# A hybrid decoder layer on one core: moving token sums, output rows, banks, norm weights and the closing order

## The chip, the core and the metric

The kernel runs on one core of one Trainium2 chip. A core has a tensor engine for matrix products (PE, with its weight loads shown apart as PEld), a vector engine (DVE), a scalar engine (ACT), a general engine (POOL) and a synchronisation engine (SP) that here only issues transfers. Each engine works through its own list of instructions in order; an instruction starts when the semaphores that it waits for are there. Transfers between main memory and the chip's memory are issued from the lists of SP, ACT and POOL. Products go into accumulation banks: eight of them, each 128 partitions by 512 float32 numbers.

The metric is the device time of one execution in microseconds (us), as the median of several runs. The times of the kernel before were 1899.18 (median of three), 1897.68 (lowest) and 1900.45 (highest).

## The reference

The reference is one layer: a token mixer with two kinds of heads, then a gated feed-forward network (FFN) with a short convolution over time, each behind a norm and added to the stream. All is float32. There are 1024 tokens of width 1024, with 16 learned tokens (`meta`) ahead that are dropped at the end. Cut to what matters:

```python
def rms_norm(x, g):
    return x * lax.rsqrt(jnp.mean(x * x, axis=-1, keepdims=True) + EPS) * g

def mixer_block(h, ...):                       # h: 1040 x 1024, normed with norm_mix
    proj = h @ w_in + b_in
    (g_q, g_k, g_v, g_r, g_lr, m_q, m_k, m_v, m_o, m_i, m_f, gate_a, gate_b) = jnp.split(proj, ...)
    log_a = jax.nn.log_sigmoid(g_lr @ gla_w_gate + gla_b_gate) / 16      # decay, per key column
    o_gla = head_rms(gla_chunked(g_q, g_k, g_v, log_a), gla_norm) * jax.nn.silu(g_r)   # 4 heads
    mq, mk = jnp.split(jax.nn.silu(causal_dwconv(concat(m_q, m_k), ml_conv_w, ml_conv_b)), 2)
    o_ml = head_rms(mlstm_chunked(mq, mk, m_v, m_i, log_sigmoid(m_f)), ml_norm) * jax.nn.sigmoid(m_o)
    y = jax.nn.sigmoid(gate_a) * (o_gla @ w_branch_gla) + jax.nn.sigmoid(gate_b) * (o_ml @ w_branch_ml)
    return y @ w_out

def conv_ffn(h, ...):                          # 2816 columns of gate and of up
    gate, up = jnp.split(causal_dwconv(h @ w_up, conv_w, conv_b), 2)
    return (jax.nn.silu(gate) * up) @ w_down

h = concat(meta, x)
h = h + mixer_block(rms_norm(h, norm_mix), ...)
h = h + conv_ffn(rms_norm(h, norm_ffn), ...)
return rms_norm(h, norm_final)[16:]
```

The two scans run over chunks of tokens; the first kind of head (GLA) decays its state per key column, the second (mLSTM) by scalar gates.

## The kernel before

**Numbers.** A float32 number is split into a rounded high part and the difference, a low part (names ending in H and L). A product of two numbers is three products: high by high, high by low, low by high. So each weight unit is loaded (`wr_`, or `raw`), rounded on ACT into `wH` and subtracted on DVE into `wL`. For the mixer this is `prep` (L104). It has two places for raw weights and three for each half. `U.get` fetches units in their order of use. `hold(ins)` makes the ACT rounding of the next units stand behind the instruction `ins` in ACT's list.

**Order.** The program is written in one stream, and a planner puts each instruction into its engine's list, by default in program order. `hp(n)` moves instructions ahead by up to n places. `tc.issue_after(ins)` puts what follows behind `ins` if it is on the same engine; that is an order, not a wait between engines. A tile with a tag shares its place with the other tiles of that tag, and a new one waits until an old one has been read.

**Start (L292 to L376).** `idle_products(8, "a")` (L338) gives PE eight products of `ident` by itself (two matrix instructions each). SP's list loads the meta rows and the first tile of x (`load_x(0, 1)`), then `norm_mix` spread over 128 partitions by the transfer itself (`gmix`, 512 KB), then the second tile of x. `norm_x(i)` (L305) norms tile i: squares with a sum on ACT, mean and root on DVE and POOL (`xr`, the root L316), one scaling by root and `gmix` on DVE (L317), eight transposes on PE (L322) in two banks, then for each bank a rounding on ACT and a subtraction on DVE into `xH` and `xL`. The squares go into a scratch tile with tag "of". After the last tile, POOL builds the masks of the scan (L379 to L407), behind the last root.

**Heads (s = 0 to 7, GLA first).** `key_query_proj` (L423) projects keys (`pk`) and queries (`pq`). For s = 0 it yields six pieces of the keys of heads 0 and 1 and the queries, then the small projection `lr` (decay and gate rows, into `raw_s`), then a piece, then `decay(0)` (L623: products, then ACT and DVE on `la` and a scan into `bc`, L637 and after), then the rest, and then puts head 0's scan `gla(0)` into the side stream, with its copies of the keys on POOL (`pk`, L712 and after). `small_rows` (L525) makes the mLSTM gate rows around head 3, with operations on few partitions by 1040 columns. `post(s)` (L585) scales a head's output and transposes it out.

**Work put beside the heads.** `token_sums(k)` (L472), k = 0 to 3, forms sums and differences of token halves for two blocks of columns: eight POOL operations of 128 by 514 in two tiles of tag "of", then eight stores of 132 KB on POOL's own queue. The gate stage (L1150 and after) reads them. It runs at the start of `post(s)` for s = 3 to 6, behind the last root on POOL. `half_load` (L501) and `half_sums` (L511) take one half of a block of `w_down`, form four differences on POOL and store them for the last stage. One half runs in each `post(s)` for s = 3 to 5, with the load behind the stores of the token sums; others in the gate stage and the merge:

```python
            for _ in range((2, 2, 1, 1, 0)[q - NK]):     # L1191, gate stage
                half_sums(*half_load(gs, "o0"))
```

**Gates, merge, output.** The merge (L1262 to L1307) multiplies the heads' outputs by the branch weights, `prod3`, in two tiles of three banks each (`big`), which DVE reads (`sb`, L1297). Then come the output products (`po`, L1520): for token tiles of 128 rows and four column blocks n of 256, `y @ w_out`. Tile 0 stands for the two rows of meta tokens that the convolution needs. `yH` and `yL` are the split rows of y, in eight blocks of 128 columns, the last of which is ready last:

```python
    for i, tiles in enumerate(([1, 5, 2, 6, 0], [3, 7, 4, 8])):
        for n in range(4):
            for u in uo[i][n]:
                U.get(u)
```

So the weights of the output (eight units of 512 KB each time) are loaded and split twice, once for each list of tiles. The first three tiles of n = 0 run together in banks X1, V0 and X0: first all but the last block of y, then the last block. `out_sum` (L1525) adds each result to the stream on DVE and squares it on ACT. At n = 3 `norm2a` norms a finished tile, and `second_norm` (L1502), which runs one or two tiles later, scales, transposes and splits it; tiles 3 and 7 and then 4 and 8 make the second piece of the FFN's tokens (`second_piece`, `combos`), whose sums and differences (L1354 to L1396) must be there before the second products of the FFN. The last `second_norm` calls stand inside the first piece of the FFN.

**FFN and end.** The up projection multiplies in seven products instead of eight, over pieces U, V, X, Y and Z (L1001). The down projection runs in rounds r and column blocks j (L1669, banks `banks[r, j, x]`). After the last of a block, `finish(r, j)` (L1745) adds the banks to the stream (`accs`), squares, roots and scales by `norm_final` (`gfin`). `whole(i)` (L1761) takes root and scaling of half a block and its store. For the end block (1, 1), the second half goes through `fo` in two column halves, the first scaled on ACT, the second on DVE, and the first half last:

```python
        nc.vector.tensor_scalar(fo[:, hi], fo[:, hi], rs, None, OP.mult)
        nc.sync.dma_start(out[P * t:P * (t + 1), hi], fo[:, hi])
        whole(0)
```

## Time and profile before

| | |
|---|---|
| median of the runs | 1899.18 us (1897.68 to 1900.45) |
| the profiled execution | 1897.74 us |
| its span in the trace | 1895.8 us |
| mean granted clock of PE | 0.996 of full speed |
| instructions | 32688 |
| read from and written to main memory | 198.33 and 69.57 MB, 141 GB/s over the span |

The profile is of one execution, with times in microseconds. A line that groups instructions names the line of the kernel, the engine, the operation, and out<-in by the program's names, then partitions x elements and types. In a list in order of time the first number is the start, the second the duration (of all x instructions that stand together), and in square brackets stand the engine's idle time just before and what ended it. A line of waits says who waited, in which group, for which engine and group, and then the total, the number and the longest. In a table of windows, the stretch is followed by its length, by the busy time of PE, PEld, DVE, ACT and POOL with the number of instructions, by the granted clock, the share of the transfer engines, and GB/s. A line for a group with three times behind it gives the shortest, the mean and the longest of one in ns, and then from when to when they ran. A busy engine is only busy; whether the time counts is told by the waits of the engine that sets the end.

### The profile page before, as it was taken

To read this page: it belongs to the slowest core of one execution; us is meant where nothing else is said; L and a number is where in the kernel's file an instruction comes from. 1 tells how busy PE (TensorE), PEld (TensorE's weight loads), DVE (VectorE), ACT (ScalarE), POOL (GpSimd) and SP (SyncE) were. 2 spreads that over 40 slices of the span, in tenths; PEclk is the share of its full clock that TensorE was granted. 3 is DMA by queue.
4 is the path that set the end of the run, shared out by engine and by line. 5 is a ranking of instruction groups with operands and counts; after the bars stand their busy time and mean duration, and the time that the engine had idled before them with its cause. 6 is when DMAs were issued, how large, how long until landed. Compare 5 with 4: busy or idle time off the path is not lost. (4 is left out here: it accounts for less than half of the span.)

```text
span 1895.8 us, 32688 instructions
## 1 busy us (share of the span) xinstructions
PE 1859.8 (98%) x13377; PEld 1779.6 (94%) x13377; DVE 1214.4 (64%) x1781; ACT 854.0 (45%) x1369; POOL 424.5 (22%) x471
## 2 busy tenths in 40 slices
PE   8999999989999999999999999999999999999998
PEld 8999999989999999999999999999999999987876
DVE  6745646455653376665442556688788788796876
ACT  5454555635543443332332325544343443465664
POOL 3201101244332001124462610012222222200000
PEclk8999999999999999999999999999999999999999
DMA  5111021062243757665883653323433334288794
GB/s 169 34 37 59 16 66 48 23 160 70 79 122 86 202 118 162 159 171 175 302 269 119 215 174 112 129 85 107 132 113 101 106 112 128 84 307 331 276 369 170
DMA packets 221824, 270.02 MB, mean 142 GB/s; under 512 B 13742, under 2 KB 177088, under 8 KB 221675
## 3 DMA queue, kind: packets, MB, share of 16 engines
q1 hardware_dynamic: 200603, 199.93, 34.8%
q0 software_dynamic: 16928, 57.76, 9.6%
q10 hardware_dynamic: 4144, 10.26, 1.5%
q8 instruction: 105, 1.72, 0.4%
q14 instruction: 44, 0.36, 0.1%
HBM read 198.33 MB, written 69.57 MB: 141 GB/s over the span
## 5 line engine op out<-in xcount | busy, mean ns | idle before, releaser
L512 POOL TENSOR_TENSOR ts<-ts 128x256 f32<-128x256 f32 x88 | 80.4, 921 | 55.8 <-DMA ts<-in_ffn_w_down_dram 53.9
L1433 POOL TENSOR_TENSOR SB<-SA,rg 128x512 f32<-128x512 f32 x20 | 32.1, 1605 | 233.8 <-issue 114.1
L206 PE MATMUL pv<-wH_mv,xH 128*128 128x256 f32 x256 | 74.9, 293 | 1.9 <-DVE v L210 1.8
L1520 PE MATMUL po<-wH_wo,yH 128*128 128x256 f32 x256 | 72.8, 285 | 2.5 <-DVE yM L1301 2.4
L206 PE MATMUL pv<-wH_gv,xH 128*128 128x256 f32 x256 | 74.7, 292 | 0.0
L206 PE MATMUL pv<-wL_gv,xH 128*128 128x256 f32 x256 | 72.0, 281 | 0.0
L206 PE MATMUL pv<-wH_gv,xL 128*128 128x256 f32 x256 | 72.0, 281 | 0.0
L1520 PE MATMUL po<-wL_wo,yH 128*128 128x256 f32 x256 | 71.7, 281 | 0.3 <-DVE wL_wo L112 0.3
L1520 PE MATMUL po<-wH_wo,yL 128*128 128x256 f32 x256 | 72.0, 282 | 0.0
L206 PE MATMUL pv<-wL_mv,xH 128*128 128x256 f32 x256 | 72.0, 281 | 0.0
L206 PE MATMUL pv<-wH_mv,xL 128*128 128x256 f32 x256 | 71.9, 281 | 0.0
L721 POOL TENSOR_TENSOR pk<-pk,kT 128x256 f32<-128x256 f32 (+1 forms) x24 | 32.8, 1368 | 147.9 <-ACT pk L719 140.3
L1468 DVE SCALAR_TENSOR_TENSOR cv<-u,fc,cv 128x1024 f32<-128x1024 f32 x44 | 65.3, 1484 | 0.4
L1415 POOL TENSOR_TENSOR A<-u2raw,A 128x512 fp32r<-128x512 f32 x20 | 43.9, 2193 | 91.8 <-ACT A L1414 91.8
L1233 PE MATMUL bg<-ogL,wH_bg 128*128 128x342 f32 x192 | 61.5, 320 | 0.0
L1233 PE MATMUL bm<-omH,wH_bm 128*128 128x342 f32 x192 | 61.4, 320 | 0.0
L1233 PE MATMUL bg<-ogH,wL_bg 128*128 128x342 f32 x192 | 61.4, 320 | 0.0
L1233 PE MATMUL bg<-ogH,wH_bg 128*128 128x342 f32 x192 | 61.4, 320 | 0.0
L1233 PE MATMUL bm<-omH,wL_bm 128*128 128x342 f32 x192 | 61.3, 319 | 0.0
L1233 PE MATMUL bm<-omL,wH_bm 128*128 128x342 f32 x192 | 61.2, 319 | 0.0
L1758 POOL TENSOR_TENSOR fr<-fv,mhalf 128x1 f32<-128x1 f32 x8 | 5.6, 711 | 226.5 <-DVE fv L1756 226.5
L210 DVE TENSOR_TENSOR v<-pv,bB 128x256 f32<-128x256 f32 x64 | 26.4, 418 | 44.1 <-PE pv L206 44.0
(754 smaller groups left out, 7518.7 us busy)
## 6 DMA issues: line engine op xcount, KB each, us to landing
gw<-in_w_in_dram SPq DMA_DIRECT2D x26, 512.0 KB
ts<-in_ffn_w_down_dram POOLq DMA_DIRECT2D x44, 256.0 KB, 3.8
tdn<-ts POOLq DMA_DIRECT2D x44, 256.0 KB, 3.5
rg<-in_ffn_w_up_dram SPq DMA_DIRECT2D x22, 512.0 KB
ru<-in_ffn_w_up_dram SPq DMA_DIRECT2D x22, 512.0 KB
adr<-s SPq DMA_DIRECT2D x40, 256.0 KB
rd<-in_ffn_w_down_dram SPq DMA_DIRECT2D x20, 512.0 KB
do<-tdn SPq DMA_DIRECT2D x18, 512.0 KB
```

The costliest lines, as they stand in the source:

```text
L206: nc.tensor.matmul(pt[:, :DV], a[:, k, t0:t0 + P], b[:, k % 4, :], start=(i == 0), stop=(i == 3 * NK - 1))
L210: nc.vector.tensor_tensor(vt[:n, c, :DV], pt[:n, :DV], bB[:n, :], OP.add)
L512: nc.gpsimd.tensor_tensor(t[:, o], t[:, a], t[:, b], OP.subtract)
L721: eng.tensor_tensor(e, e, k, OP.mult)
L1233: nc.tensor.matmul(pt[:, i, :n], a[:, k, :], b[k][:, base + t0:base + t0 + n], start=(k == 0 and j == 0), stop=(k == NK - 1 and j == 2))
L1415: eng.tensor_tensor(l, src, h.bitcast(F32), OP.subtract)
L1433: late.tensor_tensor(sb[:, 0:4], sa[:, 0:4], rg[:, 0:4], OP.subtract)
L1468: nc.vector.scalar_tensor_tensor(y, u[:, j:SEQ + j], fc[:, j, jj:jj + 1], y, OP.mult, OP.add)
L1520: nc.tensor.matmul(pt[:, :DV], a, b[:, k % 4, :], start=(k == 0 and i == 0), stop=(k == NK - 1 and i == len(terms) - 1))
L1758: nc.gpsimd.tensor_tensor(rs, v, mhalf, OP.pow)
```

## The change

It has five parts.

**Start.** `gmix` is no longer spread by a transfer. A 4 KB load of `norm_mix` into one partition (`g1`) stands first on ACT's queue, and two products of one row of ones by 512 columns of it, behind the idle products on PE, spread it over 128 partitions; DVE copies them into `gmix`. There are four idle products instead of eight. The mean of tile 2 is ordered behind the copies on DVE, the squares of tiles 3 and 4 behind the second rounding of tile 2 on ACT, and those of each later tile i behind that of tile i - 2. `prep` now puts its DVE subtraction behind the held instructions too, and the first weight unit is held behind tile 2's scaling, the second behind its rounding.

**Token sums.** The first two sets run inside `key_query_proj(0)`, behind the `lr` projection and ahead of `decay(0)` in the program, with their stores on SP's queue; the other two run in `post(4)` and `post(5)` on POOL's queue. The halves of `w_down` in `post` now run for s = 3 to 6, and the gate stage does one less.

**Banks.** Three empty tiles claim the banks V1, Y1 and Z1 ahead of the output products.

**Output rows.** The list [3, 7, 4, 8] becomes [3, 7] and [4, 8], and the units of `w_out` are loaded and split three times.

**Closing.** `whole` is split into root and `scaled`. In the second round the two scalings stand behind the sums of the block. In the end block the first half's root comes early, its sum is multiplied by `gfin` into a tile `f0`, and then scaled in two column halves, one on ACT early and one on DVE at the end, and stored from there.

The diff, cut to its core:

```diff
@@ -73,6 +73,10 @@
+    g1, ones = (hd.tile([P, T + 3], F32, name=n, tag="k", bufs=2) for n in ("g1", "ones"))
+    nc.vector.memset(ones[0:1, :P], 1.0)
+    nc.scalar.dma_start(g1[0:1, :D], bass.AP(tensor=norm_mix.tensor, offset=norm_mix.offset, ap=[[D, 1], [1, D]]))
+
     ident = const.tile([P, P], F32, name="ident")
     make_identity(nc, ident)
@@ -107,9 +111,11 @@
         wH = wp.tile(shape, F32R, name="wH_" + name, tag="wH")
         wL = wp.tile(shape, F32R, name="wL_" + name, tag="wL")
-        with tc.issue_after(held[0]) if held else nullcontext():
+        with ExitStack() as stack:
+            for ins in held:
+                stack.enter_context(tc.issue_after(ins))
             nc.scalar.activation(wH, raw, AF.Copy)
-        nc.vector.tensor_tensor(wL, raw, wH.bitcast(F32), OP.subtract)
+            nc.vector.tensor_tensor(wL, raw, wH.bitcast(F32), OP.subtract)
         return wH, wL
@@ -302,19 +308,26 @@
             xts.append(xt)
...
-    def norm_x(i):
+    def after(*ins):
+        stack = ExitStack()
+        for i in ins:
+            stack.enter_context(tc.issue_after(i.ins))
+        return stack
+
+    def norm_x(i, *order):
         n = NM if i == 0 else P
         c0 = 0 if i == 0 else NM + P * (i - 1)
...
         ss = hd.tile([P, 1], F32, name=f"xss{i}", tag="ss1", bufs=3)
         junk = hd.tile([P, T], F32, name=f"xj{i}", tag="of", bufs=2)
-        nc.scalar.activation(junk[:n, :D], xt[:n, :D], AF.Square, accum_out=ss[:n])
-        with hp(40):
+        with after(*order):
+            nc.scalar.activation(junk[:n, :D], xt[:n, :D], AF.Square, accum_out=ss[:n])
+        with hp(40), after(*order):
             v = hd.tile([P, 1], F32, name=f"xv{i}", tag="xv", bufs=3)
             nc.vector.tensor_scalar(v[:n], ss[:n], 1.0 / D, EPS, OP.mult, OP.add)
             rs = hd.tile([P, 1], F32, name=f"xr{i}", tag="xr", bufs=3)
             last = nc.gpsimd.tensor_tensor(rs[:n], v[:n], mhalf[:n], OP.pow)
-        nc.vector.scalar_tensor_tensor(xt[:n, :D], xt[:n, :D], rs[:n], gmix[:n], OP.mult, OP.mult)
+        scaled = nc.vector.scalar_tensor_tensor(xt[:n, :D], xt[:n, :D], rs[:n], gmix[:n], OP.mult, OP.mult)
         for g in range(2):
             tp = ps.tile([P, 4, P], F32, name=f"xtp{i}_{g}", tag="pj" if i == 1 else "s", bufs=3)
@@ -325,7 +338,7 @@
                 l4 = xL[:, 4 * g:4 * g + 4, c0:c0 + n]
                 nc.vector.tensor_tensor(l4, tp[:, :, :n], h4.bitcast(F32), OP.subtract)
-        return last, rounded
+        return last, rounded, scaled
...
     fc = const.tile([P, 4, 44], F32, name="fc")
@@ -339,18 +352,26 @@
         pt = ps.tile([P, P], F32, name=f"idle{name}", tag="ot", bufs=2)
         for _ in range(n):
-            nc.tensor.matmul(pt, ident, ident, start=True, stop=True)
-
-    idle_products(8, "a")
+            last = nc.tensor.matmul(pt, ident, ident, start=True, stop=True)
+        return last
+
+    idle = idle_products(4, "a")
     for dst, ap in small[:4]:
         nc.scalar.dma_start(dst, ap)
     load_x(0, 1)
-    nc.sync.dma_start(gmix, rowb(norm_mix, 0, D))
     load_x(2)
+    for i in range(2):
+        tp = ps.tile([P, 512], F32, name=f"gm{i}", tag="s", bufs=3)
+        with tc.issue_after(idle.ins):
+            nc.tensor.matmul(tp, ones[0:1, :P], g1[0:1, 512 * i:512 * i + 512], start=True, stop=True)
+        spread = nc.vector.tensor_copy(gmix[:, 512 * i:512 * i + 512], tp)
     norm_x(0)
     norm_x(1)
+    last, rounded, scaled = norm_x(2, spread)
+    made = [rounded]
+    hold(scaled.ins)
     U.get(0, 0)
-    hold(norm_x(2)[1].ins)
+    hold(rounded.ins)
     U.get(1, 0)
     hold()
@@ -359,13 +380,14 @@
     U.get(2, 0)
     columns()
-    norm_x(3)
+    made.append(norm_x(3, rounded)[1])
     load_x(6, 7, 8)
-    norm_x(4)
+    made.append(norm_x(4, rounded)[1])
     for dst, ap in small[9:]:
         nc.sync.dma_start(dst, ap)
     for i in range(5, NC + 1):
-        last, _ = norm_x(i)
+        last, rounded, _ = norm_x(i, made[i - 4])
+        made.append(rounded)
     conv_columns()
     for t, c in ((xH, 0), (xL, 32)):
@@ -433,6 +455,8 @@
                 yield from proj_cm(uk["lr"], TH_ALL, 0, lambda p, t0, n: nc.scalar.activation(
                     raw_s[0:96, t0:t0 + n], p[0:96, :], AF.Identity, bias=bsm[0:96]))
+                for k in range(2):
+                    token_sums(k, nc.sync)
                 pkq = together(pk, pq)
                 yield from islice(pkq, 1)
@@ -469,7 +493,7 @@
     tsc = [dram.tile([4, P, 4, n], F32, name=f"tsc{n}") for n in (258, 256)]
...
-    def token_sums(k):
+    def token_sums(k, queue):
...
         a, b = ([t[:, :514], t[:, 520:1034]] for t in (
@@ -490,7 +514,7 @@
         for i, src in enumerate((b[0], b[1], a[1], a[0])):
             for p in range(2):
-                stored = nc.gpsimd.dma_start(tsc[p][i, :, k], src[:, 258 * p:258 * p + 258 - 2 * p])
+                stored = queue.dma_start(tsc[p][i, :, k], src[:, 258 * p:258 * p + 258 - 2 * p])
         return stored
@@ -586,9 +610,10 @@
         h = s % 4
         g = "g" if s < 4 else "m"
-        if 3 <= s < 7:
-            with tc.issue_after(rooted[0].ins):
-                stored = token_sums(s - 3)
+        after = rooted[0]
+        if s in (4, 5):
+            with tc.issue_after(after.ins):
+                after = token_sums(s - 2, nc.gpsimd)
         for c in range(NC):
             nc.scalar.activation(o(c), o(c), AF.Copy, scale=sc[:, c + 1:c + 2])
@@ -604,9 +629,9 @@
                 if gi == 0:
                     yield
-                    if 3 <= s < 6:
+                    if 3 <= s < 7:
                         if j == 0:
-                            with tc.issue_after(stored.ins):
+                            with tc.issue_after(after.ins):
                                 t = half_load(wp, "gst")
                         else:
@@ -1188,7 +1213,7 @@
             behind_ = g
         if q >= NK:
-            for _ in range((2, 2, 1, 1, 0)[q - NK]):
+            for _ in range((2, 1, 1, 1, 0)[q - NK]):
                 half_sums(*half_load(gs, "o0"))
     next(behind_)
@@ -1220,7 +1245,7 @@
     ubm = [u_cm(w_bm, P * j, f"bm{j}") for j in range(NK)]
     uo = [[[U.add(wsrc(w_o, 4 * g, 4, DV * n, DV), [P, 4, DV], f"wo{i}{n}{g}") for g in range(2)]
-           for n in range(4)] for i in range(2)]
+           for n in range(4)] for i in range(3)]
...
     def prod3(u, X, kouter, name, ahead=2, base=0):
@@ -1535,8 +1560,11 @@
         return psF.tile([P, 512], F32, name=f"po{n}_{t}", tag=tag)
...
-
-    for i, tiles in enumerate(([1, 5, 2, 6, 0], [3, 7, 4, 8])):
+    for tag in ("V1", "Y1", "Z1"):
+        po_bank("x", tag, tag)
+
+
+    for i, tiles in enumerate(([1, 5, 2, 6, 0], [3, 7], [4, 8])):
         for n in range(4):
             for u in uo[i][n]:
@@ -1745,6 +1773,8 @@
         acc = acc_of(r, j)
         end = (r, j) == (1, 1)
+        if end:
+            f0 = rb.tile([P, T], F32, name="f0", tag="T12")[:, :D]
         ss = [const.tile([P, 2], F32, name=f"fss{r}{j}{i}", tag=f"fs{i}", bufs=2) for i in range(2)]
@@ -1758,8 +1788,7 @@
             return rs
...
-        def whole(i):
-            rs = root(i)
+        def scaled(i, rs):
             nc.vector.scalar_tensor_tensor(acc[i], acc[i], rs, gfin, OP.mult, OP.mult)
             t = 4 * i + 2 * r + j
@@ -1773,15 +1802,21 @@
             add(acc[0], hi, banks[r, j, "Y"])
             square(0, 1)
-            if not end and r:
-                whole(0)
+            if end:
+                rs0 = root(0)
+                nc.vector.tensor_tensor(f0, acc[0], gfin, OP.mult)
+                nc.scalar.activation(f0[:, lo], f0[:, lo], AF.Copy, scale=rs0)
+            elif r:
+                rs0 = root(0)
             add(acc[1], lo, banks[r, j, "Z"])
             square(1, 0)
             if not end:
                 if r:
-                    whole(1)
+                    rs1 = root(1)
+                    scaled(0, rs0)
+                    scaled(1, rs1)
                 else:
-                    later.append(whole)
+                    later.append(lambda i: scaled(i, root(i)))
                 return
         rs = root(1)
@@ -1790,7 +1825,9 @@
         nc.vector.tensor_scalar(fo[:, hi], fo[:, hi], rs, None, OP.mult)
         nc.sync.dma_start(out[P * t:P * (t + 1), hi], fo[:, hi])
-        whole(0)
+        t = 2 * r + j
+        nc.vector.tensor_scalar(f0[:, hi], f0[:, hi], rs0, None, OP.mult)
+        nc.sync.dma_start(out[P * t:P * (t + 1), :], f0)
...
     AHEAD, PRI_F = 4, 100
```

## The prediction

> **What bounds the kernel now.** I read the busy times first, then TensorE's waits, then windows and the time-ordered lists of the stages in which those waits lie.
>
> ```profile
> span 1895.8 us, 32688 instructions
> PE 1859.8 (98%) x13377; PEld 1779.6 (94%) x13377; DVE 1214.4 (64%) x1781; ACT 854.0 (45%) x1369; POOL 424.5 (22%) x471
> ```
> TensorE (PE) is busy for all but 36 us. A change that leaves its products alone can win only from those 36 us, or add to them. The waits of PE, longest first (total, times, longest):
>
> ```profile
> PE xtp L322 <- DVE xt L317: 4.2, 4, 2.7
> PE pj L163 <- DVE v L210: 2.6, 2, 1.5
> PE po L1520 <- DVE yM L1301: 2.4, 1, 2.4
> PE pv L206 <- DVE v L210: 1.8, 2, 1.0
> PE rtp L578 <- ACT of L604: 1.7, 1, 1.7
> PE sc L672 <- DVE pk L722: 1.6, 1, 1.6
> PE Vu L1001 <- DVE BL1r L1396: 1.1, 1, 1.1
> PE Xu L1001 <- ACT u2raw L1030: 0.7, 1, 0.7
> PE htp L1375 <- DVE hs L1354: 0.5, 1, 0.5
> PE Zu L1001 <- ACT BH1t L1395: 0.2, 1, 0.2
> ```
> The first row is the start, the third the first output tiles, the last four the passage to the FFN; rows two, four and five lie beside the small rows of the heads (part 2). Each part of the change aims at one of these or at the tail after the last product.
>
> The sum is made against the profiled execution: 1897.74 us, of which 1895.8 is the span. That is 1.44 us under the median 1899.18, so I add 1.44 at the end.
>
> **Part 1: norm weights by products, fewer warming products, rows in order.**
>
> ```profile
> 1.83 3.78 PE L342 MATMUL idlea<-ident 128*128 128x128 f32 x16 [1.83 <-POOL ident masks.py:199]
> 6.96 2.47 DVE L317 SCALAR_TENSOR_TENSOR xt<-xt,xr,gmix 16x1024 f32<-16x1024 f32 x2 [0.32 <-DMA gmix<-in_norm_mix_dram]
> 10.51 1.28 DVE L317 SCALAR_TENSOR_TENSOR xt<-xt,xr,gmix 128x1024 f32<-128x1024 f32 x1 [0.53 <-POOL xr L316]
> ```
> Four warming products end at 1.83 + 1.89 = 3.7 us. One of 128 columns takes 2 x 0.236 us (3.78 / 16), so a spread product of 512 columns takes about 1.9 and two 3.8: PE is through at 7.5. A copy of 512 columns on DVE is about half of a 1024-wide operation, 0.7 us: the weights stand at 8.2, 1.2 us later than now (6.96). Three scalings at some 1.2 us then end at 11.8, which is when the third ends now (10.51 + 1.28). Today the third comes 1 us after the second, for its rows land late; those come earlier when the 512 KB of spread weights no longer go ahead of them on SP's queue. What follows on DVE is the same work. The rounding of the third tile no longer stands behind the fourth tile's squares on ACT: I give that 0.2 us. The 4 KB load goes first on ACT's queue, where the first squares wait for rows anyway. The later tiles' squares now stand behind a rounding of two tiles earlier, up to 3 us later by my estimate; PE has the earlier tiles' columns to work on, so I cost it at nothing, and that cover is part of the upper bound. **-0.2**, bounds -1.5 (of the four xt waits all but the longest go, 4.2 - 2.7) and +1.5 (the 1.2 us are not caught up).
>
> **Part 2: token sums 0 and 1 move.** Now, beside the small rows:
>
> ```profile
> 372.00:390.00 18.00, 14.20 (x106) 13.27 (x104) 17.78 (x12) 7.12 (x12) 17.89 (x12) 1.00 0.03 10
> 377.19 2.23 DVE L851 SCALAR_TENSOR_TENSOR kc<-kT,col,kc 128x1040 f32<-128x1040 f32 x1
> 381.58 2.33 DVE L547 TENSOR_TENSOR sr<-sr,sr 4x1040 f32<-4x1040 f32 x1
> 390.85 1.30 DVE L851 SCALAR_TENSOR_TENSOR kc<-kT,col,kc 128x1040 f32<-128x1040 f32 x1
> 401.31 1.06 ACT L111 ACTIVATE wH_mv<-wr_mv 128x1024 fp32r<-128x1024 f32 x1 [2.06 <-DMA wr_mv<-in_w_in_dram]
> L478 POOL TENSOR_TENSOR xa<-xH,xL x12: 1282/1296/2329, 372.8 to 572.5; 128x514 f32<-128x514 f32 x12
> ```
> POOL and DVE (the columns are PE, PEld, DVE, ACT, POOL) are both full; the same DVE operation takes 2.23 us beside the sums and 1.30 after them, and a 1040-wide one 2.33 where L637 below takes 1.24. Six operations like these lose about 1 us each, 5.6 us over some 16 us of sums, and PE's waits on v (2.6 + 1.8) come behind them. The 1.7 at L578 stands behind ACT, which waits for a weight load (last but one row) that is under way together with the sums' 1 MB of stores. These 6.1 us should nearly go. What is late next: the half load now starts at once, and its four subtractions on POOL fall beside the same rows; I leave 1.3 us. **-4.8**, bounds -6.1 and -2 (the half sums and the scans of the rows keep two thirds). The sixteen stores of the two sets leave POOL's queue for SP's. In the later heads one set of sums less runs, in places where the list has no wait of PE: 0. The seventh head's added half takes POOL time that the fourth set gives up there: 0. One half less in the gate stage, where PE never waits for POOL: 0.
>
> At the first keys:
>
> ```profile
> 38.30 1.29 POOL L398 TENSOR_SCALAR_AFFINE_SELECT mfs<-mfs 128x64 f32<-128x64 f32 x2
> 61.86 1.24 DVE L637 TENSOR_TENSOR la<-bc,la 128x1040 f32<-128x1040 f32 x1 [3.06 <-ACT la L636]
> 67.09 2.08 POOL L712 COPY pk<-kT 128x256 f32<-128x256 f32 x2 [27.49 <-ACT kT L420]
> 68.36 0.38 SPq L107 DMA_DIRECT2D wr_gq<-in_w_in_dram  x1
> 73.79 1.13 PE L672 MATMUL sc<-pk 128*128 128x128 f32 x8 [1.65 <-DVE pk L722]
> 77.14 1.05 ACT L111 ACTIVATE wH_gq<-wr_gq 128x1024 fp32r<-128x1024 f32 x1
> ```
> POOL is free for 27.5 us. Two sets of eight operations at 1.29 us are 20.6 us. The masks are held behind the last tile's root, which comes about 4 us later (part 1), so they end nearer 44 than 39.6, and the second set ends at 64 to 65, beside DVE's decay chain that begins at 61.86 and for which PE already waits 1.65 us. About 4 us of sums beside it, at the loss seen above (5.6 in 16), cost **+1.5**; bounds 0 (done by 61.8) and +5 (the second set waits until the first one's stores have left its rows, runs to 70 and holds up the copies of 67.09 as well). The 16 stores go on SP. Behind them stands the weight load of 68.36, which may slip by some microseconds: it is split at 77.14, so 0.
>
> **Part 3: banks.**
>
> ```profile
> 1102.78 1.23 DVE L1297 TENSOR_TENSOR sb<-bm,sb 128x1026 f32<-128x1026 f32 x1 [2.88 <-PE bm L1233]
> 1115.81 0.51 DVE L1297 TENSOR_TENSOR sb<-bm,sb 128x342 f32<-128x342 f32 x1
> 1116.46 0.36 PE L1520 MATMUL po<-wH_wo,yH 128*128 128x256 f32 x1 [2.39 <-DVE yM L1301]
> 1118.65 1.29 DVE L1305 TENSOR_TENSOR yL<-sb,yH 128x512 fp32r<-128x512 f32 x2 [0.70 <-ACT yH L1304]
> ```
> PE starts right after DVE's third read of the last merge product (1115.81 + 0.51), out of the three banks that the first tiles take. With V1, Y1 and Z1 claimed ahead, these tiles get the next three, which DVE has read by 1104. Their first 63 products use no last row of yH and take 63 x 0.118 = 7.4 us (price in part 4); the last row is split by 1120, so nothing is late next. **-2.35**, bounds -2.4 and 0 (the banks stay).
>
> **Part 4: output rows two by two.** Eight more weight units: each a 512 KB load, one ACT and one DVE operation.
>
> ```profile
> L111 ACT ACTIVATE wH_wo<-wr_wo x16: 1042/1046/1065, 1091.7 to 1208.3; 128x1024 fp32r<-128x1024 f32 x16
> L112 DVE TENSOR_TENSOR wL_wo<-wr_wo,wH_wo x16: 1203/1214/1225, 1093.8 to 1209.4; 128x1024 fp32r<-128x1024 f32 x16
> 1175.00:1223.00 48.00, 47.18 (x400) 46.70 (x399) 33.56 (x54) 23.88 (x51) 2.52 (x4) 1.00 0.44 138
> PE po L1520 <- DVE wL_wo L112: 0.3, 1, 0.3
> ```
> A product costs PE 47.18/400 = 0.118 us, a tile of 24 products 2.83, a pair 5.7. With three places for each weight half, a pair's second unit can be split only when the unit three before it is free, 1.4 us ahead of the handoff, and it is wanted 1.4 us behind it: 2.8 us for 1.05 on ACT, 1.21 on DVE and the signals. So a handoff has about 0.3 us to spare. The ones of before cost 0.3 us all together. But DVE goes from 33.6 to 33.6 + 8 x 1.21 = 43.3 of 48 us, so that an operation of 0.7 to 1.3 us is often ahead. I take 0.4 us for each of the seven closer handoffs, less the 0.3: **+2.5**; bounds 0 and +10.5 (1.5 each, a whole operation ahead on DVE and part of one on ACT). In return tiles 3 and 7 are normed while 4 and 8 are multiplied. That takes those tiles' scalings, halvings of differences and subtractions, by the durations above about 8 us, from DVE in the passage, whose waits of PE are 1.1 + 0.7 + 0.5 + 0.2 = 2.5. They should go but for 0.5, since the first FFN weights are split later than before: **-2.0**, bounds -2.5 and 0.
>
> **Part 5: closing.**
>
> ```profile
> 1884.12 2.25 PE L1669 MATMUL pdZ<-do,dy 128*128 128x512 f32 x9
> 1890.01 0.49 DVE L1791 TENSOR_SCALAR fo<-fo,fr 128x512 f32<-128x512 f32 x1 [0.66 <-POOL fr L1758]
> 1890.57 1.28 DVE L1763 SCALAR_TENSOR_TENSOR accs<-accs,fr,gfin 128x1024 f32<-128x1024 f32 x1
> ```
> PE ends at 1886.37; behind it stand a sum, squares, a root and two scalings, then a store. The last scaling shrinks from 1.28 to 0.49 (-0.8), but a multiplication of 1.2 us enters DVE's queue earlier, and one half of it a scaling on ACT, where the last squares must not stand behind it. The two scalings of the block before move behind its sums. **-0.3**, bounds -0.9 and +1.2 (the multiplication stands ahead of the last sum).
>
> **Sum:** -0.2 - 4.8 + 1.5 - 2.35 + 2.5 - 2.0 - 0.3 = -5.65: 1892.1 for the profiled execution, **1893.5** as a median.
>
> **Rivals.**
> *The keys take it back.* DVE's decay chain pays the full +5 instead of +1.5: -2.15, 1897.0. For it: PE waits there already. Against: 27 us of idle POOL. The Trainium skill, "SBUF — State Buffer", section "SBUF: two separate sides", says that DVE operations with two SBUF inputs and GpSimd lock each other out for a whole instruction; the 2.23 against 1.30 us agrees.
>
> *The weights bind (slower).* At the pair handoffs of part 4 the stall is 1.5 us each: 7 x 1.5 - 2.5 = +8, and the passage gains nothing, +2: 1893.5 + 10 = 1903.5. It decides from 1.43 us a handoff. For it: DVE would be at 90% in this stage. Against: the handoffs of before cost 0.3 in all.
>
> *The banks do not move.* Claiming empty tiles shifts nothing: 1893.5 + 2.35 = 1895.9.
>
> *The clock stays up.*
>
> ```profile
> 8.00:10.00 2.00, 1.18 (x11) 1.09 (x12) 1.72 (x4) 1.15 (x2) 0.08 (x1) 0.78 1.19 313
> 18.00:20.00 2.00, 2.00 (x13) 2.00 (x13) 1.27 (x3) 0.00 (x0) 0.55 (x1) 0.66 1.03 418
> ```
> With a clock of 1 or 0.5, the means 0.78 and 0.66 (the last column but two) put the fall at 9.1 and the return at 19.4. The dense products, from about 15.7 on, run at half rate for 3.7 us; spread products that bridge the idle time before 8 us could save that half, 1.8: 1891.7. The Trainium skill, "TensorE: Matmul & The Clock Gate", Part 1, has PE's activity judged in free-running windows of about 3.4 us; 19.4 - 9.1 is three of them. By that rule fewer warming products could as well leave it cold longer.
>
> **How the numbers follow.** Runs of this kernel tell about 0.2%, 3.8 us, from no change: faster is under 1895.4, slower over 1903.0. Forecast 0.46 and clock 0.08 make faster 0.54. Keys 0.15, banks 0.07 and smaller misses at the start, the close and the handoffs 0.05 make 0.27 within. Weights 0.19 are slower. All bounds at once would reach from 1885.8 to 1915.4; I take 1888 to 1904, which leaves out the upper half of the weights case, 0.1, and 0.05 below. The forecast's own range is 1889.5 to 1895.4.
>
> **What would show it.** Part 1: the first dense key product starts within 0.5 us of where it does now. Part 2: PE's waits on v (L210) fall under 1.5 us in all, DVE is back at 1.3 us beside the small rows, and the sc wait near 72 us is about 3 us. Part 3: the 2.4 us wait at the first output tile is gone. Part 4: PE's waits on wL_wo total 2 to 3 us, those on the second token piece (L1395, L1396) under 0.6. Part 5: 9.2 us instead of 9.4 from the last product to the end of the span. I am wrong if the wL_wo waits pass 6 us, the sc wait passes 5, or the first output tile still waits for the merge.

## The result, and the profile after

The changed kernel takes 1903.96 us (median of ten runs, 1902.51 to 1909.33), the kernel before 1899.39 (1897.68 to 1901.88): a ratio of 1.0027, 95% interval 1.0017 to 1.0036. It is slower by 0.27%, where 1893.5 was forecast; the time lies just inside the stated range (1888 to 1904) and far above the forecast's own (1889.5 to 1895.4). The profiled execution of the changed kernel took 1904.08 us, with a span of 1902.4; that is 6.6 us more span than before.

The page's first lines:

```profile
span 1902.4 us, 32743 instructions
PE 1863.4 (98%) x13373; PEld 1781.3 (94%) x13373; DVE 1212.3 (64%) x1793; ACT 862.0 (45%) x1378; POOL 409.4 (22%) x455
```

PE's longest waits, with total, number and longest:

```profile
PE ftp L348 <- DVE fc L349: 6.4, 1, 6.4
PE xtp L335 <- DVE xt L330: 4.2, 4, 2.2
PE htp L1400 <- DVE hn L1385: 2.8, 2, 2.0
PE idlea L355 <- POOL ident masks.py:199: 1.8, 1, 1.8
PE Vu L1026 <- ACT BH1r L1420: 1.7, 1, 1.7
PE sc L697 <- DVE pk L747: 1.7, 1, 1.7
PE ot L627 <- ACT of L629: 1.6, 1, 1.6
PE po L1545 <- DVE wL_wo L118: 1.5, 3, 0.8
```

Three things are gone as forecast: the waits on v (2.6 + 1.8), the one at the small rows (1.7) and the one at the first output tile (2.4). The list has a new head: 6.4 us for a copy into `fc`, a small table of the FFN's convolution weights that nobody would look for on the path. And `htp` now waits 2.8 us for `hn`, where the passage to the FFN had waited 2.5 in all.

Waits do not add up to 6.6 us, so I compared when PE starts the same product in both traces. How much later the changed kernel is:

```
product                                     before     after    later by
first key product                            13.88     14.56      0.68
106th key or query product                   36.71     38.39      1.68
121st                                        38.49     48.93     10.44
first product of the scan (sc)               73.79     85.35     11.56
head 3, just before the small rows          319.05    330.64     11.59
first product of the mLSTM scan (msc)       426.15    430.38      4.23
first gate product (Vg)                     658.73    662.80      4.07
first product of the last b gates (pe)      921.04    926.23      5.19
first output product (po)                  1116.46   1119.10      2.64
553rd output product                       1187.28   1189.81      2.53
FFN, 89th product of piece V               1296.66   1302.76      6.10
first down product                         1670.91   1677.02      6.10
last down product                          1885.98   1892.57      6.58
```

So the change loses 11.6 us within the first 50, wins 7.4 beside the small rows and 2.6 at the first output tile, and loses 3.6 between the output rows and the FFN. The steps of 1.1 us in the gate stage and 0.5 in the down projection do not stand in every run below: a run with the same gate stage has the first at 0.0, and waits of the down projection on ACT's `dy` come and go from run to run (0 to 1.3 us) without a change there. I take both for chance, without having shown it.

The loss lies at 40 us. DVE there in the kernel before, with the copies into `fc` (the first is shown) ahead of the casts (CAST) of the scan's masks:

```profile
36.17 0.24 DVE L336 COPY fc<-ftp 128x88 f32<-128x88 f32 x1
...
37.82 1.27 DVE L402 CAST mu<-mfs 128x128 uint8<-128x128 f32 x4
39.63 0.23 DVE L402 CAST mu<-mfs 128x128 uint8<-128x128 f32 x1 [0.54 <-POOL mfs L398]
```

And DVE in the changed kernel:

```profile
41.50 0.35 DVE L424 CAST mu<-mfs 128x128 uint8<-128x128 f32 x1 [0.97 <-POOL mfs L420]
43.22 0.45 DVE L424 CAST mu<-mfs 128x128 uint8<-128x128 f32 x1 [1.36 <-POOL mfs L420]
44.01 0.67 DVE L424 CAST mu<-mfs 128x128 uint8<-128x128 f32 x1 [0.34 <-POOL mfs L420]
46.71 0.23 DVE L424 CAST mu<-mfs 128x128 uint8<-128x128 f32 x1 [2.04 <-POOL mfs L420]
46.86 0.24 DVE L349 COPY fc<-ftp 128x88 f32<-128x88 f32 x1
47.02 1.28 DVE L340 TENSOR_TENSOR xL<-xtp,xH 128x512 fp32r<-128x512 f32 x2
```

The casts now wait for POOL, one after the other. Behind them in DVE's list, and ready long since, stand the copy into `fc` and the splits of the last token tile. POOL's roots in the kernel before (the last two), then POOL at this place in the changed kernel, then PE, then windows around it:

```profile
27.82 1.97 POOL L316 TENSOR_TENSOR xr<-xv,mhalf 128x1 f32<-128x1 f32 x2 [1.61 <-DVE xv L314]
```

```profile
36.38 0.55 POOL L329 TENSOR_TENSOR xr<-xv,mhalf 128x1 f32<-128x1 f32 x1 [2.48 <-DVE xv L327]
```

```profile
47.16 0.41 PE L348 MATMUL ftp<-ident,vf 88*128 88x88 f32 x1 [6.45 <-DVE fc L349]
```

```profile
44.00:46.00 2.00, 0.00 (x0) 0.00 (x0) 0.67 (x1) 0.00 (x0) 2.00 (x4) 0.64 0.00 0
46.00:48.00 2.00, 0.84 (x4) 0.85 (x5) 1.29 (x4) 0.00 (x0) 0.90 (x3) 0.50 0.00 0
48.00:50.00 2.00, 2.00 (x12) 2.00 (x11) 0.45 (x2) 0.47 (x1) 1.92 (x2) 0.50 0.04 8
```

The last tile's root (`xr`) starts at 36.38, where it started at 29.25 before, and POOL is done with the masks at 46.7 instead of 39.6. While PE waits, the granted clock (the last column but two) falls to one half. By half-microsecond windows it falls at 44.6 and is back at 51.4, so PE's first 4.2 us of products after the wait run at half speed. The wait of 6.45 and half of 4.2 make 8.6 of the 9.9 us that are lost from here on; 1.7 were lost ahead of it.

### The profile page after: what moved, and what is told of

It reads as the page before. It is cut to its first block, busy times and chain, and to the rows that moved or that the text cites. A ratio compares the mean times of both kernels' runs of the same rounds, so it can differ in the third digit from the quotient of the medians.

```text
span 1902.4 us, 32743 instructions
## 1 busy us (share of the span) xinstructions
PE 1863.4 (98%) x13373; PEld 1781.3 (94%) x13373; DVE 1212.3 (64%) x1793; ACT 862.0 (45%) x1378; POOL 409.4 (22%) x455
## 4 chain that ended last, share of the span: by engine, by line
PE 84%; DVE 7%; DMA 3%; ACT 2%; issue 2%; POOL 1%; SPq 0%; DVEq 0%; ACTq 0%; POOLq 0%
PE pj L169 11%; PE pv L212 7%; PE Zu L1026 6%; PE Xu L1026 6%; PE Yu L1026 6%; PE bg L1258 5%; PE bm L1258 5%; PE Xg L1026 4%; PE Yg L1026 4%; PE Zg L1026 4%; PE Vu L1026 3%; PE po L1545 3%; PE pdX L1697 2%; PE pdY L1697 2%; PE pdZ L1697 2%; PE Vg L1026 2%
```

## The experiments

My theory after these readings: **the order of the squares** in the start makes roots and masks late, the planner then puts DVE's casts ahead of the `fc` copies, and everything else in the change works about as forecast. The rival: the **token sums on POOL**, which run from 32 to 68 us there, hold up DVE and the masks. The four runs of the first set tell these apart, and the pairs of output rows with them.

**Masks behind the copies.** In the edit, `fixed` is the second copy into `fc`, which `conv_columns` now returns:

```diff
-    with tc.issue_after(last.ins):
+    with tc.issue_after(last.ins), tc.issue_after(fixed.ins):
         lmask = {}
```

> The changed kernel, with one order added: what builds the masks of the scan (on POOL and DVE) stands behind the two copies into fc and with them behind the splits of the last token tile in DVE's list; nothing is left out. In the profile of the changed kernel PE waits 6.45 us at 40.7 us for a copy into fc, and five DVE casts of masks stand ahead of that copy; POOL is done with the masks 7 us later than before. Theory (order): the casts wait for POOL, the copy waits behind the casts, and the granted clock falls to one half after this wait; together they make the step from 1.7 us late (106th key product) to 11.5 us. Then this run is 9 to 10 us faster than the changed kernel, about 1894 us, the wait at L348 is under 1 us and the clock stays at 1.0 from 22 us on. Rival (sums): the token sums that now run on POOL beside the keys hold up DVE; then the lateness at the first score product stays near 11.5 us and the time near 1904.

Measured: 1898.17 us, 0.999 of before (0.9981 to 0.9999): 5.8 us won against the changed kernel, not 9 to 10. The wait at L348 is gone and the lateness at 60 us is 3.6 us instead of 11.5. But at the scan it grows again, to 5.7 us at the first product and 6.9 a few microseconds later. PE now comes there 8 us earlier, and there DVE's decay chain runs beside the last token sums on POOL. DVE of this run, and then its POOL:

```profile
65.50 2.26 DVE L663 TENSOR_TENSOR la<-bc,la 128x1040 f32<-128x1040 f32 x1 [3.07 <-ACT la L662]
67.80 3.31 DVE L664 TENSOR_TENSOR_SCAN bc<-rmask,la 128x1040 f32<-128x1040 f32 x1
```

```profile
65.36 1.30 POOL L506 TENSOR_TENSOR xb<-xb 128x514 f32<-128x514 f32 x1
66.74 2.18 POOL L506 TENSOR_TENSOR xa<-xa,xb 128x514 f32<-128x514 f32 x1
```

Each of the two DVE operations takes 1.0 us longer than before (1.24 and 2.32). PE's wait for `pk` is 3.67 us instead of 1.65, and the clock falls behind it (from 79.7 to 83.1 us), for 1.3 us more. That is the rival "the keys take it back" of the prediction, at 2.0 to 3.3 us; in the changed kernel itself it costs nothing, because PE was so late that the sums were done at 68.4 and the chain began at 73.4. So one delay had hidden another. Both theories hold a part: the order is worth 7.9 us, the sums 3.3 where the order is mended.

**The squares in no order.**

```diff
-    last, rounded, scaled = norm_x(2, spread)
+    last, rounded, scaled = norm_x(2)
...
-    made.append(norm_x(3, rounded)[1])
+    made.append(norm_x(3)[1])
...
-        last, rounded, _ = norm_x(i, made[i - 4])
+        last, rounded, _ = norm_x(i)
```

> The changed kernel without the order of the squares and means of tiles 2 to 8 behind earlier roundings and copies; nothing is left out. Theory (order): with the squares early again, the last root is back near 30 us, the masks are made 6 to 7 us earlier, and the planner puts the copies into fc ahead of the casts; the wait of 6.45 us and the second fall of the clock go: about 1894 us. Rival (sums): the token sums are still beside the keys, so the time stays near 1904.

Measured: 1895.64 us, 0.9976 (0.9967 to 0.9985). In DVE's list the copies stand ahead of the casts again, the `fc` wait is gone, and the time falls by 8.3 us with the sums where they are: the theory stands. What is left of the start is 3.5 us of lateness, and it comes early, with a wait of 6.4 us at 8 us. The first scalings come later still, at 13.2 us, and DVE's list shows why. The mean of tile 3 (`xv`) now stands ahead of them; it waits for that tile's squares on ACT, which wait until 11.8 us for its rows:

```profile
13.09 0.15 DVE L327 TENSOR_SCALAR xv<-xss 128x1 f32<-128x1 f32 x1 [3.82 <-ACT xj L324]
13.21 2.47 DVE L330 SCALAR_TENSOR_TENSOR xt<-xt,xr,gmix 16x1024 f32<-16x1024 f32 x2
```

So without the order another instruction stands in DVE's way; this run takes one loss out and puts a smaller one in.

**The token sums back.** `token_sums(0..3)` and the half sums as in the kernel before.

```diff
-                for k in range(2):
-                    token_sums(k, nc.sync)
...
-        if s in (4, 5):
+        if 3 <= s < 7:
             with tc.issue_after(after.ins):
-                after = token_sums(s - 2, nc.gpsimd)
+                after = token_sums(s - 3, nc.gpsimd)
```

> The changed kernel with the token sums and half sums where they were in the kernel before (post of heads 3 to 6); nothing is left out. Theory (order): the first 60 us stay as in the changed kernel, 11 us late, with the wait for fc of about 6 us, since DVE's list there is the same; and the waits beside the small rows come back, 7.3 us: about 1911 us. Rival (sums): the first 60 us lose some 10 us, the waits beside the small rows come back: about 1901 us.

Measured: 1912.23 us, 1.0063 (1.0049 to 1.0076), and PE waits 6.45 us for `fc` at 39.8 us, with no sum near it. The sums as the cause of the loss are out. Their move is worth 8.3 us by the medians, a little more than the 7.3 read from the trace.

**The output rows together** (on the run with the masks behind).

```diff
-    for i, tiles in enumerate(([1, 5, 2, 6, 0], [3, 7], [4, 8])):
+    for i, tiles in enumerate(([1, 5, 2, 6, 0], [3, 7, 4, 8])):
...
-           for n in range(4)] for i in range(3)]
+           for n in range(4)] for i in range(2)]
```

> As the run with the masks behind, and the output tiles 3, 7, 4 and 8 in one list again with the weights split twice; nothing is left out. Theory (weights and norms): the list in pairs costs 1.3 us more at the handoffs and 2.3 us more in the passage to the FFN (lateness 2.5 us at 1187 us, 6.1 us from 1297 us on), so this run is 3 to 4 us under the run with the masks behind, about 1890.5. Rival (noise of placing): the passage's waits come from the first FFN weights alone and stay; then the gain is 1 to 1.5 us.

Measured: 1895.44 us, 0.998 (0.9971 to 0.9989), 2.7 us less than with pairs; behind the passage it is 3.0 us ahead of that run. The pairs cost a little less than the 3 to 4 us expected. Where, is read from DVE of the changed kernel at the end of the first pair:

```profile
1201.48 0.15 DVE L1379 TENSOR_REDUCE hs<-hss 128x1 f32<-128x4 f32 x1
1201.54 1.22 DVE L1421 TENSOR_TENSOR BL<-T,BH 128x1024 fp32r<-128x1024 f32 x1
1202.68 1.22 DVE L118 TENSOR_TENSOR wL_wo<-wr_wo,wH_wo 128x1024 fp32r<-128x1024 f32 x1
1203.81 0.42 DVE L1552 TENSOR_TENSOR h<-po,h 128x256 f32<-128x256 f32 x1
1205.90 1.23 DVE L118 TENSOR_TENSOR wL_wo<-wr_wo,wH_wo 128x1024 fp32r<-128x1024 f32 x1 [1.68 <-ACT wH_wo L117]
1207.05 0.42 DVE L1552 TENSOR_TENSOR h<-po,h 128x256 f32<-128x256 f32 x1
1207.38 0.14 DVE L1381 TENSOR_SCALAR hv<-hs 128x1 f32<-128x1 f32 x1
...
1208.25 1.28 DVE L1385 SCALAR_TENSOR_TENSOR hn<-h,hr,gffn 128x1024 f32<-128x1024 f32 x1 [0.47 <-POOL hr L1383]
```

The sum of squares of tile 3 (`hs`) is there at 1201.6; the next step, `hv`, stands 5.8 us later in the list, behind two weight splits and two output sums. PE reaches the transposes that want `hn` at 1207.6 and waits 2.0 us. Of some 3.2 us, 1.2 are handoffs (1.5 against 0.3), about 2 this wait, and the rest the passage, which did not get shorter: its waits are 0.3 + 0.7 + 1.7 + 0.2 now, 2.5 before.

The second set starts from the start of before, to see what the other parts are worth without the first.

**The first part undone** (spread by the transfer, eight idle products, `norm_x` and `prep` of before, the rest as changed).

> The changed kernel with its first part undone (norm weights spread by the transfer, eight idle products, squares and weight splits in the order of before); nothing is left out. Theory (order of the squares): the start is that of before, so the first key products come within 0.5 us of before, the masks are made by about 41 us, the token sums are done by 62 us, when DVE's decay chain begins, and cost nothing there; the waits beside the small rows (7.3 us) and at the first output tile (2.5) stay gone; the pairs of output rows cost 3.5. Sum against before: 0 - 7.3 - 2.5 + 3.5 = -6.3, about 1893 us. Rival (sums beside the decay chain): the sums run past 62 us and hold up DVE's chain as they did with the masks behind (2.0 us more wait for the first scores, and 1.3 us from the slower clock behind it): about 1896 us.

Measured: 1891.55 us, 0.9953 (0.994 to 0.9967), and the lateness at the scan's first product is 0.4 us. The same two DVE rows in this run, and the last sum on POOL:

```profile
62.25 1.24 DVE L651 TENSOR_TENSOR la<-bc,la 128x1040 f32<-128x1040 f32 x1 [3.06 <-ACT la L650]
63.53 2.33 DVE L652 TENSOR_TENSOR_SCAN bc<-rmask,la 128x1040 f32<-128x1040 f32 x1
```

```profile
59.04 1.30 POOL L494 TENSOR_TENSOR xa<-xa,xb 128x514 f32<-128x514 f32 x1
```

The sums end at 60.3, two microseconds ahead of the chain, and cost nothing. The first part of the change thus costs 12.4 us by the medians, and 11.2 by the lateness at the scan's first product (11.6 less 0.4).

**The rows together too** (`b_start_undone` with the edit of the rows).

> As the run before it in this list, and the output tiles 3, 7, 4 and 8 in one list again: only the token sums, the banks and the closing order of the change are left. Nothing of the computation is left out. Theory: the pairs cost 3.5 us, so 3 to 4 us less than the run with the first part undone, about 1889.5 us, under both kernels. Rival: with the start of before the passage has other cover and the pairs are worth their weights; then no change or slower.

Measured: 1889.44 us, 0.994 (0.9928 to 0.9953), 2.1 us less. By the lateness the pairs cost 3.2 again up to 1214 us; here the clock fell in the passage and gave 1.5 back (last section).

**The norms later.**

```diff
-                if hn and len(hn) == 2 or hn and n < 3:
+                if (hn and len(hn) == 2 or hn and n < 3) and (i, n) != (2, 0):
                     second_norm()
```

> As the run with the first part undone, but the scaling, transposes and splits of output tiles 3 and 7 come one column block later, behind the second pair of products of tiles 4 and 8; nothing is left out. Theory (norms right behind the products): the wait of 1.8 to 2.0 us for hn at the first of these transposes comes from the root chain of tile 3 behind weight splits and sums in DVE's list; with a block of cover it is gone: 1.8 us less than the run with the first part undone. Rival: the work only moves, and the passage's last waits (0.3 + 0.7 + 1.7) grow by as much.

Measured: 1894.12 us, 0.9964 (0.995 to 0.9978), against 1891.55 no gain. PE's waits there:

```profile
PE po L1534 <- DVE wL_wo L112: 2.9, 4, 1.0
...
PE Yu L1015 <- DVE LSA L1429: 1.3, 1, 1.3
...
PE htp L1389 <- DVE hn L1374: 0.9, 1, 0.9
```

The 2.2 us for the first `hn` are gone, but the handoffs grow from 1.3 to 2.9 and one wait of the passage from 0.2 to 1.3: by the lateness the stretch costs 3.2 us as before. (In its profiled execution 1.5 us more lies in the gate stage.) The rival is right that the work only moved, though more of the wait went to the handoffs than to the passage. What is short here is DVE, as I read it; the window of the changed kernel has it busy for 43.1 of 48 us, the most beside PE:

```profile
1175.00:1223.00 48.00, 44.33 (x369) 43.24 (x368) 43.11 (x60) 32.34 (x61) 1.92 (x3) 1.00 0.59 177
```

**The banks undone** (on the run with start and rows undone).

```diff
-    for tag in ("V1", "Y1", "Z1"):
-        po_bank("x", tag, tag)
```

> As the run with start and rows undone, without the three empty tiles that claim banks; nothing is left out. Theory (banks): the first output tile waits for DVE's last read of the merge again, 2.4 us more. Rival: the gain of 2.5 us at this place came from the order of DVE's splits of y, not from the banks: no change.

Measured: 1893.3 us, 0.9962 (0.9949 to 0.9976), 3.9 us more; and the old wait is back, alone:

```profile
PE po L1534 <- DVE yM L1315: 2.4, 1, 2.4
```

The lateness steps by 2.55 us at this place in every run with the three empty tiles, and by 0 here. Of the rest, 1.5 us in this profile come right behind that wait, where the granted clock is at one half from 1113.05 to 1116.46. Another 1.5 come from such a stretch at 160.7 us, which the edit does not touch. How much of this the other runs had stays open; the profiled execution, 1895.66 us, is the slowest of the four.

**The spread by load** (on the run with the masks behind) splits the first part in two.

```diff
-    idle = idle_products(4, "a")
+    idle = idle_products(8, "a")
...
     load_x(0, 1)
+    nc.sync.dma_start(gmix, rowb(norm_mix, 0, D))
     load_x(2)
-    for i in range(2):
-        tp = ps.tile([P, 512], F32, name=f"gm{i}", tag="s", bufs=3)
...
```

> As the run with the masks behind, and the norm weights spread by the transfer again, with eight idle products; the squares and the weight splits keep the order of the change. Nothing is left out. Theory (order of the squares): what makes the first 60 us late, 3.65 us with the masks behind, is the order: PE waits 0.5 + 0.5 + 1.3 us for the scaled tiles 5 to 8; so the lateness at 60 us stays at 2.5 to 4 us, and the time at about 1898. Rival (the products that spread the weights): the lateness comes from the spread, which sets the first scaling 1.5 us later; then the lateness falls under 1.5 us and the time to 1895 or less, the sums being done earlier too.

Measured: 1895.52 us, 0.9972 (0.9962 to 0.9983), 2.6 us less than with the products. The lateness at 60 us is 0.8 instead of 3.6. Here my theory missed: with the masks mended, more of the remaining loss is the spread by products (2.8 us) than the order (from 0.4 early to 0.8 late behind the waits for tiles 5 to 8). Both are of one trace each, and the lateness of the first 60 us differs by up to 1 us either way among runs with one and the same start (last section). The sums still run past 62 us and cost 1.4 us of wait and 1.3 of slower clock.

**The closing undone too** (start, rows and closing as before; `finish` of the kernel before).

> As the run with start and rows undone, and the closing order of before: only the token sums and the banks of the change are left. Nothing of the computation is left out. Theory: the closing order is worth 0.05 to 0.1 us of the time behind the last product (9.46 against 9.39 to 9.41 us), so no difference that can be told. Rival: it is worth 0.3 us or more.

Measured: 1888.29 us, 0.994 (0.9923 to 0.9957): no difference from 1889.44 that can be told. The time behind the last product is 9.42 against 9.39 us. SP's last stores in the kernel before and then in the changed one:

```profile
1890.52 0.33 SPq L1792 DMA_DIRECT2D out_dram<-fo  x1
1891.88 0.33 SPq L1765 DMA_DIRECT2D out_dram<-accs  x1
```

```profile
1897.24 0.33 SPq L1830 DMA_DIRECT2D out_dram<-f  x1
1897.66 0.38 SPq L1827 DMA_DIRECT2D out_dram<-fo  x1
```

DVE is done 4.6 us behind the last product (at 1897.54, the product at 1892.95) instead of 5.5 (1886.37 to 1891.85), but the span ends 4.7 us behind SP's last store instead of 3.9. The first of the last stores starts no earlier behind the last product, 4.3 us instead of 4.15, and the two of SP start within 0.4 us instead of 1.4. The transfer engines are full after that in both kernels: their share is 1.03 from 1892 to 1893 us before, and 0.98 from 1898 to 1899 in the changed kernel. So the gain on DVE is lost behind the stores. That the transfers of the last 1 MB (ACT stores a quarter of it) set the end is my reading; no run tests it.

This kernel, with the token sums and the banks alone, is by its median the fastest of the study, 0.6% under the kernel before and 0.8% under the changed one.

## Why the prediction was wrong

The sum was -5.65 us, and the span grew by 6.6. Of the 12.2 us between them, 11.75 are part 1.

**Part 1** (-0.2, bounds -1.5 to +1.5) is the step that failed. "The later tiles' squares now stand behind a rounding of two tiles earlier, up to 3 us later by my estimate; PE has the earlier tiles' columns to work on, so I cost it at nothing". PE had columns, and was only 1.7 us late by the 106th product. But the last root came 7.1 us later, and what hangs on the root is not PE's columns alone. In part 2 I did follow the masks, "about 4 us later", and asked only what POOL would do behind them. (The two figures, up to 3 and about 4 us, do not agree with each other, and both are too small.) I did not ask who takes the masks: DVE, in order, with copies and splits behind the casts for which PE waits. That is 7.9 us of lateness by the run with the masks behind, the clock's fall among it. The spread itself cost 2.8 us where I had the 1.2 us caught up. DVE's first scalings in the changed kernel:

```profile
8.52 2.48 DVE L330 SCALAR_TENSOR_TENSOR xt<-xt,xr,gmix 16x1024 f32<-16x1024 f32 x2
...
11.32 1.28 DVE L330 SCALAR_TENSOR_TENSOR xt<-xt,xr,gmix 128x1024 f32<-128x1024 f32 x1
```

The first begins 1.6 us later than before and the third 0.8, behind splits of the first tile that now lie between; I had the third where it was.

**Part 2** (-4.8, bounds -6.1 to -2) is right in its mechanism and too small: 7.35 us. The waits' rows hold 6.3, with one of 0.2 for `ot` that is not in the prediction's list; the rest, up to 0.3 us at each of the six, no row shows (PE's first product after a wait also takes longer, 0.39 against 0.28 us at a handoff). My upper bound stopped at the rows. And the 1.3 us that I left for the half load did not come: none of the four groups waits any more, and DVE is back at 1.30 us for the operation that took 2.23 (L876 at 387.2 us), as forecast.

**First keys** (+1.5, bounds 0 to +5): 0 in the changed kernel, 0 with the start of before, 2.0 and 1.3 us of slower clock with the masks mended. The mechanism and the point from which it is paid, DVE's chain, were right.

**Part 3** (-2.35): 2.55, right.

**Part 4**: handoffs +2.5 were 1.2, passage -2.0 was about +2.3. I had reckoned that norms taken out of the passage would free it; they were put into a stretch where DVE is 90% busy (43.1 of 48 us, against 43.3 forecast), and the root chain of tile 3 lay 5.8 us in its list. The work did leave the passage, and PE waited for it elsewhere.

**Part 5** (-0.3): -0.05. I priced DVE and ACT and left the stores out.

In the lateness, 11.55 at the keys, -7.35 at the small rows, -2.55 at the banks and 3.6 in the output and the passage make 5.25; 1.1 in the gate stage and 0.5 in the down projection, of which I said that they come and go, less 0.3 in small steps, make it the 6.6 us of the span.

Among the rivals, "the weights bind" gives about the measured time, 1903.5, and is wrong: the handoffs cost 1.5 us in all, not 10.5. The range reached up to 1904 for this rival, so that the time lies inside it is luck. "The keys take it back" is a true mechanism that another delay covered. "The clock stays up" did not come: PE's dense products run at half speed from 17.25 to 20.67 us, 3.4 us, where the prediction had 3.7 before.

## What to carry to other kernels

When an order or a wait makes an early step later, follow every consumer of that step on each engine, and ask in each in-order list what stands right behind it; the price is paid by the bystanders (here two copies of 0.24 us). A delay can hide another: mend the first, and look again at what then collides. And work moved out of a stage is worth its price only if the stage that takes it has room on that engine.

## What the runs showed that I had not expected

The granted clock falls and returns in steps of 3.4 us. By the clock's record the slow stretches are 10.24 us before (9.1 to 19.4), 3.4 and 6.8 us in the changed kernel (17.25 to 20.67, 44.56 to 51.39), 3.4 and 3.4 with the masks behind. Each trace also begins at half speed. The windows show 1.00 ahead of the record's first entry, but that is no reading of the clock: without the order of the squares the first entry is at 18.56 us, sixteen transposes of 128 columns take 3.33 us at 15.7 us, and eight take 1.04 at 24.4.

Whether the clock falls isn't set by the length of a wait alone. PE waits 2.39 us for the merge in the kernel before (until 1116.46) and, with the banks undone, again (until 1112.03). These are windows 2 us behind that wait, of the kernel before and then of the run with the banks undone:

```profile
1118.00:1120.00 2.00, 2.00 (x19) 2.00 (x19) 1.29 (x2) 1.13 (x2) 0.00 (x0) 1.00 0.62 165
1114.00:1116.00 2.00, 2.00 (x11) 2.00 (x11) 1.29 (x2) 0.70 (x2) 0.00 (x0) 0.50 0.77 246
```

The first keeps its clock; the second loses it for 3.4 us and with it 1.5 us of time. In the run with start and rows undone it is lost in the passage, where no wait near is over 1.14 us, for 3.4 us from 1230.3 on and again 1.5 us of time; the kernel before has the same waits there and keeps it.

The Trainium skill, "TensorE: Matmul & The Clock Gate", Part 1, says that the windows of 3413 ns run freely, whatever the kernel does; the stretches agree, for in each of the twelve traces all changes of the clock lie whole windows of 3.41 us apart. I cut the traces into these windows. Until shortly before the last product, the clock fell behind windows in which PE was busy for 0 to 2.2 of the 3.4 us, and it never stayed up behind one with less than 1.65; between the two figures both happen. So the same kernel gains or loses 1 to 2 us by where its waits fall among these windows, which may well be much of the spread between the runs (1897.7 to 1901.9 us before). The start shows it too: five runs have the start of before, and at the 121st product they are from 1.0 us early to 0.9 us late. The full clock comes at 13.96 us in the earliest of them and at 20.78 in the latest (19.4 before).

The price of DVE beside POOL is whole operations: 2.26 against 1.24 and 3.31 against 2.33 us, 1.0 more each. The Trainium skill, "SBUF — State Buffer", section "SBUF: two separate sides", has GpSimd and a DVE operation with two SBUF inputs, as both of these are, lock each other out for an instruction. The 1.0 us more is near one sum's 1.3 us.
